# Six re-read buffers and six kept gelus, a shared pool for attention's keys, and row fetches moved between stages of a decoder layer

## The chip, the cores and the metric

The kernel runs on one core of a Trainium2 chip. The metric is the time of one execution on the device, in microseconds (us). Engines are named as in the profile: PE (matrix multiplication), DVE (vector), ACT (activation), POOL (GpSimd) and SP (which here only issues DMAs); POOL issues the indirect DMAs.

## The reference

One layer of a decoder for 512 new tokens of a prompt and 64 tokens of eight running sequences: a gated short convolution and a sliding-window attention, merged through sigmoid gates, layer norm, and then a mixer that picks 128 of 16,384 experts for each token:

```python
def block_fn(xb):                                    # a block of tokens, h
    qv = einsum('nd,de->ne', xb, w_pq).reshape(PEER_BLOCK, 8, 2, 128)
    s = einsum('nhpc,hpkc->nhpk', qv, sub_keys)      # two lists of 128 key scores per head
    top_s, top_i = top_k(s, 16)
    cand_s = top_s[:, :, 0, :, None] + top_s[:, :, 1, None, :]
    cand_i = top_i[:, :, 0, :, None] * 128 + top_i[:, :, 1, None, :]
    best_s, sel = top_k(cand_s.reshape(PEER_BLOCK, 8, -1), 16)
    idx = take_along_axis(cand_i.reshape(PEER_BLOCK, 8, -1), sel)
    gate = softmax(best_s)
    pre = einsum('nd,nhkd->nhk', xb, expert_u[idx])
    coef = gate * gelu(pre)
    return einsum('nhk,nhkd->nd', coef, expert_v[idx])

y = layer_norm(ALPHA * h + peer(h), ln2_g, ln2_b)
```

All arithmetic is in float32; matrix products use a high and a low part of each operand and three products (hi times hi, hi times lo, lo times hi).

## The kernel before

**Tiles.** The 576 token rows lie in chunks of 128: chunk 0 (prompt rows 0 to 127), `SMP` (the 64 sample rows and prompt rows 128 to 191), and chunks 1 to 3 (the other 320 prompt rows). Chunk 0 and `SMP` form the first half, chunks 1 to 3 the second; for the mixer the 64 prompt rows of `SMP` are moved into the free half of chunk 3.

**Two ways through the experts.** For chunk 0 and the 64 sample rows (`GATHER`) the chosen expert rows are fetched: one indirect DMA of 128 rows of 1024 values (512 KB) for each of 192 slots (128 experts for each row of chunk 0, and 64 slots that hold two experts for each sample row), issued by POOL (L512), first 192 from `expert_u`, each followed by a dot product on DVE (L526), then 192 from `expert_v`, each followed by a multiply-add on DVE (L535). `experts()` is a generator; one step issues the fetch that lies `GLAG` steps ahead, into one of `GBUF` row buffers, and does one DVE operation. It is called as side work: `table(..., pace)` loads a 512 KB table on SP (L138), copies the high part on ACT (L119), subtracts it on POOL or DVE to get the low part `wlo` (L120), and, if `pace` is over 0, runs `pace` steps of the generator behind that subtraction. For the other 384 token rows (`DENSE`) all 16,384 experts are computed, in 128 tables. `front(t)` (L856) loads table t of `expert_u`, multiplies it with the transposed activations (24 matmuls of 128x384) and applies gelu on ACT; for t < `NS` the result goes through a tile `sp` to DRAM (`spill`), for later t it is kept in a tile `gel` of `LAG` buffers. `middle(t)` (L898) multiplies it on DVE (L910) with the gate values `gm` (loaded eight tables at a time in three DMAs of 512 KB); for t < `NS` the spilled gelu is first read back into a tile `re` (three buffers, L905); then ACT and DVE make its high and low part, `chi` and `clo`. `back(t)` loads table t of `expert_v`, and 18 matmuls of 128x512 (L940) add to six accumulators in PSUM.

**Stages.** (1) To about 520 us: projections, convolution, attention, merge and first layer norm of both halves, the first half's key scores and routing among them. (2) Scores of the second half, four groups of four `w_pq` tables with top-16 searches and routing on DVE (`route`, with an Exp on ACT, L448), each followed by five fronts (`FQ`), to 780 us. (3) Gate matrices: `hot` tiles (one-hot rows times weights: compare on DVE, L787, scale on ACT, L793, or POOL, L795; matmul L796), with fronts between groups until `AHEAD - KEEP` are done; to about 905 with fronts and to 978 without. (4) The last ten fronts ahead of the sweep (`KEEP`), 978 to 1033. (5) The sweep: steps t < `NS` hold only second products ("solo", to 1290), while `AHEAD` = `NS + LAG` fronts were done ahead; then each step has 18 second-product matmuls and a front's 24 ("paired", to 1777); the fronts run out `LAG` steps before the end, and the rest is solo again (the tail). (6) Second layer norm of chunks 1 to 3 and the output.

**What sets the order.** Nothing moves at run time: the framework simulates the program once and writes each engine's instructions in the order in which that simulation started them, so a change of buffer counts or of paces can move instructions in every queue. SP's queue and POOL's are in that order too. `tc.issue_after` holds an instruction behind another one. The paces are constants: none behind tables of the second half's scores (L586), two or one in turn behind fronts before the sweep (`PACE_U`), none behind fronts in the sweep, one behind each `back` for t < `NS` and three afterwards (`PACE_V`). The first products' low parts are made on POOL before the sweep and on DVE in it; the second products' on DVE for t < `NS` and for t over 124, on POOL between.

## Time and profile before

| | us |
|---|---|
| median of 3 runs (lowest, highest) | 1848.39 (1845.89, 1849.37) |
| the profiled execution | 1850.18 |
| its span in the trace | 1848.4 |
| PE busy (93%) | 1723.9 |
| weight loads on PE, beside matmuls (85%) | 1566.4 |
| DVE busy (79%) | 1464.7 |
| ACT busy (42%) | 781.4 |
| POOL busy (60%) | 1109.6 |

The profiled execution's own time is 1.8 us over its span. The shares are means over stages that are not alike, so the table only says which engine to look at first; the rows below divide the span by stage. The DMA engines moved 496.50 MB, 269 GB/s on the mean, and the granted PE clock was 0.972 of full speed.

### The profile page before, as it was taken

To read this page: it belongs to the slowest core of one execution; us is meant where nothing else is said; L and a number is where in the kernel's file an instruction comes from. 1 tells how busy PE (TensorE), PEld (TensorE's weight loads), DVE (VectorE), ACT (ScalarE), POOL (GpSimd) and SP (SyncE) were. 2 spreads that over 40 slices of the span, in tenths; PEclk is the share of its full clock that TensorE was granted. 3 is DMA by queue.
4 is the path that set the end of the run, shared out by engine and by line. 5 is a ranking of instruction groups with operands and counts; after the bars stand their busy time and mean duration, and the time that the engine had idled before them with its cause. 6 is when DMAs were issued, how large, how long until landed. Compare 5 with 4: busy or idle time off the path is not lost.

```text
span 1848.4 us, 27569 instructions
## 1 busy us (share of the span) xinstructions
PE 1723.9 (93%) x9760; PEld 1566.4 (85%) x9760; DVE 1464.7 (79%) x2588; ACT 781.4 (42%) x1337; POOL 1109.6 (60%) x724
## 2 busy tenths in 40 slices
PE   7999998998799999899888899999999999999985
PEld 7998898988489899799878778778999999999974
DVE  5634579998965699987893778779788878888887
ACT  4554444443233344377794333333333333343322
POOL 4445434367857777798645422224678787778783
PEclk9999999999989999899999999999999999999998
DMA  7446443368757789899748899999999999989873
GB/s 252 134 150 225 138 132 122 115 200 300 249 201 241 235 294 311 271 349 348 289 188 303 317 333 335 336 346 339 333 314 345 337 324 350 353 307 343 314 268 104
DMA packets 190539, 496.50 MB, mean 269 GB/s; under 512 B 17712, under 2 KB 83696, under 8 KB 187312
## 3 DMA queue, kind: packets, MB, share of 16 engines
q1 hardware_dynamic: 135104, 293.39, 46.5%
q0 software_dynamic: 55296, 201.35, 30.2%
q8 instruction: 76, 1.25, 0.3%
q14 instruction: 63, 0.52, 0.1%
HBM read 454.48 MB, written 40.54 MB: 268 GB/s over the span
## 4 chain that ended last, share of the span: by engine, by line
PE 40%; DVE 23%; DMA 14%; issue 9%; POOL 8%; ACT 4%; SPq 1%; DVEq 0%; POOLq 0%; ACTq 0%
PE acc L940 15%; PE ps L123 7%; PE ps L124 7%; PE ps L125 7%; DMA g<-in_ev,idx 5%; POOL wlo L120 4%; POOL g L512 4%; DVE junk L526 3%; PE ps L796 3%; DMA re<-spill 2%; DVE wlo L120 2%; DMA raw<-in_ev 2%; DMA raw<-in_w_o 1%; ACT whi L119 1%; ACT hot L793 1%
## 5 line engine op out<-in xcount | busy, mean ns | idle before, releaser
L120 POOL TENSOR_TENSOR wlo<-raw,whi 128x1024 fp32r<-128x1024 f32 x232 | 579.1, 2499 | 301.8 <-ACT whi L119 264.7
L119 ACT ACTIVATE whi<-raw 128x1024 fp32r<-128x1024 f32 x388 | 409.5, 1056 | 603.9 <-PE ps L124 236.1
L123 PE MATMUL ps<-xhi,whi 128*128 128x384 f32 (+2 forms) x1600 | 529.9, 331 | 21.6 <-ACT sp L863 13.4
L125 PE MATMUL ps<-xhi,wlo 128*128 128x384 f32 (+2 forms) x1600 | 526.1, 329 | 3.5 <-POOL wlo L120 2.0
L124 PE MATMUL ps<-xlo,whi 128*128 128x384 f32 (+2 forms) x1600 | 526.1, 329 | 0.0
L535 DVE SCALAR_TENSOR_TENSOR h<-g,pre,h 128x1024 f32<-128x1024 f32 x192 | 309.8, 1614 | 68.3 <-DMA g<-in_ev,idx 66.8
L512 POOL DMA_INDIRECT g<-in_eu,idx x192 | 204.2, 1063 | 233.1 <-DVE junk L526 186.9
L123 PEld LDWEIGHTS ps<-xhi,whi 128*128 128x128 f32 x1600 | 308.4, 193 | 31.0 <-ACT sp L863 15.1
L512 POOL DMA_INDIRECT g<-in_ev,idx x192 | 257.0, 1338 | 124.9 <-DVE h L535 77.9
L125 PEld LDWEIGHTS ps<-xhi,wlo 128*128 128x128 f32 x1600 | 307.8, 192 | 5.3 <-POOL wlo L120 2.3
L124 PEld LDWEIGHTS ps<-xlo,whi 128*128 128x128 f32 x1600 | 308.3, 193 | 2.9 <-issue 0.3
L940 PE MATMUL acc<-whi,chi 128*128 128x512 f32 x756 | 291.4, 392 | 14.5 <-ACT chi L119 8.2
L940 PE MATMUL acc<-wlo,chi 128*128 128x512 f32 x756 | 296.9, 393 | 7.6 <-POOL wlo L120 7.6
L940 PE MATMUL acc<-whi,clo 128*128 128x512 f32 x756 | 256.4, 392 | 1.1 <-DVE clo L120 1.1
L120 DVE TENSOR_TENSOR wlo<-raw,whi 128x1024 fp32r<-128x1024 f32 x156 | 203.5, 1304 | 46.0 <-ACT whi L119 43.6
L940 PEld LDWEIGHTS acc<-whi,chi 128*128 128x128 f32 x756 | 142.6, 189 | 46.7 <-ACT chi L119 11.5
L940 PEld LDWEIGHTS acc<-wlo,chi 128*128 128x128 f32 x756 | 142.4, 188 | 38.0 <-POOL wlo L120 9.7
L526 DVE SCALAR_TENSOR_TENSOR junk<-g,hp 128x1024 bf16<-128x1024 f32 x104 | 125.9, 1210 | 56.8 <-DMA g<-in_eu,idx 54.8
L940 PEld LDWEIGHTS acc<-whi,clo 128*128 128x128 f32 x756 | 142.4, 188 | 31.3 <-DVE clo L120 1.6
L526 DVE SCALAR_TENSOR_TENSOR junk<-g,h 128x1024 bf16<-128x1024 f32 x88 | 130.9, 1488 | 3.3 <-DMA g<-in_eu,idx 3.0
L796 PE MATMUL ps<-hot 128*128 128x128 f32 x768 | 113.4, 290 | 14.5 <-ACT hot L793 13.4
L787 DVE TENSOR_TENSOR hot<-pt,T 128x1024 f32<-128x1024 f32 x96 | 113.9, 1218 | 15.8 <-PE ps L796 12.7
(250 smaller groups left out, 2157.9 us busy)
## 6 DMA issues: line engine op xcount, KB each, us to landing
raw<-in_euT SPq DMA_DIRECT2D x128, 512.0 KB
raw<-in_ev SPq DMA_DIRECT2D x128, 512.0 KB
gd<-gb SPq DMA_DIRECT2D x24, 1024.0 KB
gm<-gd SPq DMA_DIRECT2D x48, 512.0 KB
raw<-in_w_g SPq DMA_DIRECT2D x32, 512.0 KB
raw<-in_w_pq SPq DMA_DIRECT2D x32, 512.0 KB
raw<-in_w_bch SPq DMA_DIRECT2D x24, 512.0 KB
spill<-sp SPq DMA_DIRECT2D x60, 192.0 KB
```

The lines of the kernel that those rows point to most:

```text
L119: A.activation(hi, src, AF.Copy)
L120: return (eng or V).tensor_tensor(lo, src, hi.bitcast(F32), op=ALU.subtract)
L123: PE.matmul(ps, L[0], R[0], start=start, stop=False)
L124: PE.matmul(ps, L[0], R[1], start=False, stop=False)
L125: PE.matmul(ps, L[1], R[0], start=False, stop=stop)
L512: G.indirect_dma_start(out=rows[i], out_offset=None, in_=I[src], in_offset=bass.IndirectOffsetOnAxis(ap=idx[c][:, s:s + 1], axis=0))
L526: V.scalar_tensor_tensor(junk, g, 1.0, in_psum(c), op0=ALU.mult, op1=ALU.mult, accum_out=p)
L535: V.scalar_tensor_tensor(h_tok[c], g, p, h_tok[c], op0=ALU.mult, op1=ALU.add)
L787: V.tensor_tensor(hot, iota_ps.unsqueeze(1).unsqueeze(1).broadcast_to([128, 2, 4, 128]), T[:, 0:2, n:n + 4].unsqueeze(3).broadcast_to([128 ...
L793: A.activation(oi, oi, AF.Copy, scale=weight_of)
L796: newest[1] = PE.matmul(ps[:, r * 128:(r + 1) * 128], hot[:, 1, r, :], oi, start=True, stop=True).ins
L940: PE.matmul(*args, **kw)
```

## The change

- `NS` 60 to 63 and `LAG` 9 to 6: 63 gelus are spilled and six kept; `AHEAD` stays at 69, so the same fronts run before the sweep, and in the sweep a front runs six tables ahead of its second product. `re` gets six buffers.
- `GBUF` 4 to 5, `GLAG` 2 to 3: five row buffers, fetches three ahead. `OB` 3 to 4: four `hot` buffers.
- Paces: one step behind each `w_pq` table of the second half's scores (`PACE_Q`); three behind each of the last ten fronts before the sweep; for t < `NS` one step behind two of three `back` calls. After `NS` they stay at three.
- `mask_p`, `kT_all` and `v_all` (1, 2 and 2.5 KB a partition) move from the constants to a pool of their own, which is closed after attention, so that later pools can use the room; the scores' `sc` tiles get a pool that is closed before the gate matrices.

```diff
-NS = 60
-LAG = 9
+NS = 63
+LAG = 6
 AHEAD = NS + LAG
-GBUF = 4
-GLAG = 2
+GBUF = 5
+GLAG = 3
...
-OB = 3
+OB = 4
...
-PACE_A, PACE_B, PACE_U, PACE_V = (1, 0), (2, 1, 1), (2, 1), (1, 3)
+PACE_A, PACE_B, PACE_Q, PACE_U, PACE_V = (1, 0), (2, 1, 1), 1, (2, 1), (1, 3)
...
-    mask_p = const("mask_p", [128, 256], src=I["mask_p"])
...
-    kT_all = const("kT_all", [128, SEQ])
-    v_all = const("v_all", [128, 5, 128])
...
         if s.units > LO_N:
-            return table(src, "w", G)
+            return table(src, "w", G, PACE_Q)
...
+    kvs = ExitStack()
+    pools["kv"] = kvs.enter_context(pool("kv", "right"))
+    mask_p, kT_all = tmp("kv", [128, 256], "mask_p"), tmp("kv", [128, SEQ], "kT_all")
+    v_all = tmp("kv", [128, 5, 128], "v_all")
+    loads.insert(0, (mask_p, I["mask_p"]))
...
+    kvs.close()
...
-    pools["b"] = bs.enter_context(pool("b", "right"))
+    pools["b"] = bs.enter_context(pool("b0", "right"))
...
-        wu = table(I["euT"][t], "w", G if t < AHEAD else V, PACE_U[t % len(PACE_U)] if t < AHEAD else 0)
+        wu = table(I["euT"][t], "w", G if t < AHEAD else V, (PACE_U[t % len(PACE_U)] if t < AHEAD - KEEP else 3) if t < AHEAD else 0)
...
+    bs.close()
+    pools["b"] = bs.enter_context(pool("b", "right"))
...
-            ge = tmp("v", [128, ND], "re", bufs=3)
+            ge = tmp("v", [128, ND], "re", bufs=6)
...
-                   PACE_V[t >= NS])
+                   PACE_V[1] if t >= NS else PACE_V[0] * (t % 3 > 0))
```

The change moves line numbers: the dot is L523 after, the fetch L509, the re load L911, the compare L784.

POOL's queue at the end of the sweep, before; each `wlo` is the low part of one second-product table, the last one that of table 124, and each `g<-in_ev` a row fetch:

```order
L512 DMA g<-in_ev,idx_98 128x1024 x3
L120 TENSOR_TENSOR wlo<-raw,whi 128x1024
L512 DMA g<-in_ev,idx_98 128x1024 x3
L120 TENSOR_TENSOR wlo<-raw,whi 128x1024
L512 DMA g<-in_ev,idx_98 128x1024 x3
L120 TENSOR_TENSOR wlo<-raw,whi 128x1024
L512 DMA g<-in_ev,idx_98 128x1024 x3
L120 TENSOR_TENSOR wlo<-raw,whi 128x1024
L512 DMA g<-in_ev,idx_98 128x1024
L120 TENSOR_TENSOR wlo<-raw,whi 128x1024
L512 DMA g<-in_ev,idx_98 128x1024 x3
L120 TENSOR_TENSOR wlo<-raw,whi 128x1024 x2
```

and after, again to table 124:

```order
L509 DMA g<-in_ev,idx_95 128x1024 x3
L120 TENSOR_TENSOR wlo<-raw,whi 128x1024
L509 DMA g<-in_ev,idx_95 128x1024 x3
L120 TENSOR_TENSOR wlo<-raw,whi 128x1024
L509 DMA g<-in_ev,idx_95 128x1024 x3
L120 TENSOR_TENSOR wlo<-raw,whi 128x1024
L509 DMA g<-in_ev,idx_95 128x1024 x3
L120 TENSOR_TENSOR wlo<-raw,whi 128x1024
L509 DMA g<-in_ev,idx_95 128x1024 x2
L120 TENSOR_TENSOR wlo<-raw,whi 128x1024 x4
```

The last fetch stands ahead of the last four tables' subtractions instead of the last two, with two or three fetches in a step up to there. Beside this PE's order has the last front's matmuls ahead of table 118's second products before, and ahead of table 121's after.

POOL's queue around the last group of four `w_pq` tables of the second half's scores, before (the five `wlo` in a row are theirs and that of the front behind them; `g<-in_eu` are row fetches for the dots):

```order
L512 DMA g<-in_eu,idx_95 128x1024
L120 TENSOR_TENSOR wlo<-raw,whi 128x1024
L512 DMA g<-in_eu,idx_95 128x1024 x2
L120 TENSOR_TENSOR wlo<-raw,whi 128x1024 x5
L512 DMA g<-in_eu,idx_95 128x1024
L120 TENSOR_TENSOR wlo<-raw,whi 128x1024
L512 DMA g<-in_eu,idx_95 128x1024 x2
L120 TENSOR_TENSOR wlo<-raw,whi 128x1024
```

and after:

```order
L509 DMA g<-in_eu,idx_92 128x1024 x2
L120 TENSOR_TENSOR wlo<-raw,whi 128x1024
L509 DMA g<-in_eu,idx_92 128x1024
L120 TENSOR_TENSOR wlo<-raw,whi 128x1024
L509 DMA g<-in_eu,idx_92 128x1024
L120 TENSOR_TENSOR wlo<-raw,whi 128x1024
L509 DMA g<-in_eu,idx_92 128x1024
L120 TENSOR_TENSOR wlo<-raw,whi 128x1024
L509 DMA g<-in_eu,idx_92 128x1024
L120 TENSOR_TENSOR wlo<-raw,whi 128x1024
L509 DMA g<-in_eu,idx_92 128x1024
L120 TENSOR_TENSOR wlo<-raw,whi 128x1024
```

A fetch now follows each of these tables, here and in the three groups ahead. On DVE the dots that stand ahead of the first `hot` compare go from 92 to 112 with all that moves, ahead of the last from 128 to 151, and ahead of the third top-16 batch of the second half's scores from 53 to 66. The fetches issued from the last front before the sweep to the first second-product table that POOL splits (table 60, now 63) go from 68 to 56.

SP's queue in the solo part of the sweep, around the fourth block of three `gm` loads, before:

```order
L138 DMA raw<-in_ev 128x1024 x2
L906 DMA re<-spill 128x384 x3
L138 DMA raw<-in_ev 128x1024 x2
L902 DMA gm<-gd 128x8x128 x3
L906 DMA re<-spill 128x384 x2
L138 DMA raw<-in_ev 128x1024
L906 DMA re<-spill 128x384
L138 DMA raw<-in_ev 128x1024 x2
L906 DMA re<-spill 128x384
```

and around the same block after:

```order
L138 DMA raw<-in_ev 128x1024
L911 DMA re<-spill 128x384
L138 DMA raw<-in_ev 128x1024
L907 DMA gm<-gd 128x8x128 x2
L911 DMA re<-spill 128x384
L907 DMA gm<-gd 128x8x128
L138 DMA raw<-in_ev 128x1024
L911 DMA re<-spill 128x384
L138 DMA raw<-in_ev 128x1024
L911 DMA re<-spill 128x384
```

Where that block's first load stands, 25 loads of `expert_v` tables and 17 of `re` have been issued before, 20 and 16 after; at the next block 33 and 26 before, 28 and 24 after. In ACT's order of the ten fronts ahead of the sweep, where the first `expert_v` tables are copied too, five gelus stand ahead of the first two table copies that follow each other directly before, and seven after.

## Rows read from the trace of the kernel before

**Rows 1.** Windows: stretch and length, busy us (instructions) of each engine, PEclk, DMA share, GB/s.

```profile
520.00:625.00 105.00, 104.85 (x649) 101.03 (x649) 53.06 (x225) 37.89 (x55) 76.95 (x46) 1.00 0.73 245
625.00:780.00 155.00, 139.30 (x786) 136.16 (x785) 152.72 (x495) 62.30 (x85) 114.24 (x70) 0.95 0.82 278
...
780.00:905.00 125.00, 123.72 (x832) 123.14 (x831) 104.00 (x128) 90.47 (x219) 108.69 (x100) 0.99 0.95 347
905.00:978.00 73.00, 59.82 (x395) 52.97 (x395) 67.29 (x69) 64.81 (x188) 31.20 (x52) 0.95 0.50 201
978.00:1033.00 55.00, 45.12 (x247) 44.34 (x245) 22.23 (x23) 18.07 (x25) 30.30 (x18) 0.93 0.89 303
1033.00:1290.00 257.00, 248.46 (x1079) 203.47 (x1080) 205.69 (x308) 88.93 (x118) 73.06 (x65) 0.99 0.97 338
1290.00:1777.00 487.00, 487.00 (x2461) 443.07 (x2460) 414.05 (x355) 174.94 (x239) 373.71 (x228) 1.00 0.93 329
1777.00:1848.00 71.00, 44.02 (x183) 33.40 (x182) 56.66 (x67) 18.50 (x28) 37.40 (x22) 0.90 0.48 162
```

**Rows 2.** Chain near 1300 (start us, us, what), then PE's timeline in the tail.

```profile
1295.72 4.12 PE acc L940 x18
...
1304.03 4.12 PE acc L940 x18
...
1777.35 0.39 PE L940 MATMUL acc<-whi,chi 128*128 128x512 f32 x1
...
1830.65 0.39 PE L134 MATMUL acc<-whi,sp 128*128 128x512 f32 x1
```

**Rows 3.** Waits of PE, 1777 to 1832: total us, times, longest us.

```profile
PE acc L940 <- POOL wlo L120: 7.6, 5, 2.9
```

**Rows 4.** Timeline of POOL in the tail: start us, us, instruction [idle before <-releaser].

```profile
1801.15 2.42 POOL L120 TENSOR_TENSOR wlo<-raw,whi 128x1024 fp32r<-128x1024 f32 x1
1803.72 1.76 POOL L512 DMA_INDIRECT g<-in_ev,idx  x1 [0.16 <-issue]
1805.79 1.00 POOL L512 DMA_INDIRECT g<-in_ev,idx  x1 [0.30 <-issue]
1807.09 1.36 POOL L512 DMA_INDIRECT g<-in_ev,idx  x1 [0.30 <-issue]
```

**Rows 5.** Lines by form, 1050 to 1250 (busy us, mean ns | idle before), then PE's waits.

```profile
L940 PE MATMUL acc<-whi,chi 128*128 128x512 f32 x280 | 109.8, 392 | 8.0 <-ACT chi L119 8.0
...
L512 POOL DMA_INDIRECT g<-in_eu,idx x46 | 46.2, 1004 | 149.7 <-DVE junk L526 149.7
L910 DVE TENSOR_TENSOR re<-re,gm 128x384 f32<-128x384 f32 x45 | 24.8, 554 | 27.2 <-DMA re<-spill 27.2
...
PE acc L940 <- ACT chi L119: 8.2, 8, 1.6
```

**Rows 6.** Lines by form, 650 to 780; waits of DVE, 520 to 625; of PE, 620 to 780.

```profile
L526 DVE SCALAR_TENSOR_TENSOR junk<-g,hp 128x1024 bf16<-128x1024 f32 x35 | 42.1, 1203 | 0.0
...
L526 DVE DVE_READ_ACCUMULATOR junk<-g,hp 128x1 f32 x35 | 2.7, 77 | 0.0
...
DVE junk L526 <- DMA g<-in_eu,idx: 50.4, 9, 14.3
...
PE ps L123 <- ACT sp L863: 13.4, 4, 6.3
```

**Rows 7.** Waits of PE, 905 to 1033: total us, times, longest us.

```profile
PE ps L796 <- ACT hot L793: 12.1, 20, 2.4
```

**Rows 8.** Timelines of PE and DVE, 1010 to 1035.

```profile
1012.80 0.69 PE L123 MATMUL ps<-xhi,whi 128*128 128x384 f32 x1 [4.85 <-ACT gel L867]
...
1033.31 0.77 PE L940 MATMUL acc<-whi,chi 128*128 128x512 f32 x1 [5.34 <-ACT whi L119]
...
1014.40 1.92 DVE L910 TENSOR_TENSOR re<-re,gm 128x384 f32<-128x384 f32 x1 [10.17 <-DMA re<-spill]
```

**Rows 9.** Timeline of DVE, 1809 to 1831: the last accumulations of fetched rows.

```profile
1810.13 6.77 DVE L535 SCALAR_TENSOR_TENSOR h<-g,pre,h 128x1024 f32<-128x1024 f32 x3 [2.02 <-DMA g<-in_ev,idx]
```

## The prediction, as put on record

> **What bounds the kernel now.** I read first the busy times by stretch [rows 1]. One engine carries most of the time, PE, and it is not loaded alike everywhere: from 1290 to 1777 us it is busy 487.00 of 487.00 us, so no edit can shorten that stretch without taking matmuls away, and this change takes none. What can move is in six other places. From 625 to 780 DVE is busy 152.72 of 155 us and PE loses 15.7. From 780 to 905 PE is nearly full (123.72 of 125). From 905 to 978 the gate matmuls wait for ACT. From 978 to 1033 ten fronts take 55 us. From 1033 to 1290 PE is busy 248.46 of 257 us beside a DMA share of 0.97. After 1777 PE is busy 44.02 of 71 us. Then I read, for those stretches only, what PE waits for, and last the rows of the engine that it waits for: a wait "on POOL" in the tail is a question of what else POOL does there.
>
> **The tail: gain 11 (3 to 13).** The last front ends at 1777.35 and PE's last matmul at 1831.04 [rows 2]: 53.7 us for ten table steps of second products. A step that nothing hinders is 18 matmuls in 4.12 us [rows 2], ten are 41.2, so 12.5 are lost. The waits name POOL's subtraction for 7.6 of it [rows 3]; the rest goes in smaller stops around those. Why POOL is late stands in its rows: ahead of a subtraction of 2.4 us lie three row fetches of 1.00 to 1.76 us [rows 4], so a step costs POOL about 1.76 + 1.00 + 1.36 + 0.8 between them + 2.4 = 7.3 us, where PE needs 4.12. In the paired stretch PE takes 8.31 us for a step (1304.03 - 1295.72, [rows 2]), and the same 7.3 fit. The change moves exactly this: with LAG 6 the last front stands ahead of table 121 instead of 118, so the run of steps without fronts shrinks from ten to seven, and the order shows the last fetch ahead of POOL's last four subtractions instead of its last two. All steps with three fetches then lie beside fronts. The three steps that leave the tail are not gone: they stand at the head of the sweep (64 solo steps there instead of 61), where POOL splits nothing. Of 12.5 I leave 2 (tables 125 to 127 are split on DVE, and the sample chunk's finish now stands near them in ACT's and DVE's queues) and count the end after PE's last matmul, 17 us of the span, unchanged. Upper end 13, lower end 3 where the finish gets in the way (a rival, below).
>
> **Solo steps with spilled gelus: gain 7 (3 to 9.5).** From 1050 to 1250 one of the three kinds of product ran 280 times [rows 5], six to a step: 46.7 steps in 200 us, 4.286 us each, 0.166 above 4.12. Over 60 steps that is 10. PE's waits there are eight on ACT's chi, 8.2 us together [rows 5], one for every eight steps, which is when three loads of gm (512 KB each) go out on SP's queue. Chi is late because DVE's multiplication waits 27.2 us in that window for re [rows 5], and re's load stands behind gm on the one queue with at most three buffers ahead. With six buffers the order puts more re loads ahead: where the fourth block of gm is issued, 25 ev and 17 re have been issued before, 20 and 16 now, and in the next block 28 and 24; re trails ev by four instead of eight, so each re has about four steps (16 us) more than it had, against 4.7 us for three gm loads at 338 GB/s (1.57 MB). Does the bandwidth carry it? Per step: 512 KB of ev, 192 of re, 192 of gm (1536 over eight steps), and 46 fetches of 512 KB in 46.7 steps [rows 5]: 1400 KB, or 334 GB/s at 4.286 us, against 338 shown. After, 56 fetches are issued in 64 steps instead of 68 in 61 (two in three back steps carry one): 1344 KB per 4.12 us is again 334, and with the bare pace of two in three 1237 KB is 307. So the freed fetches are what pays for the faster step. I take 7 of 10 and not all of it, because the DMA share of 0.97 is a second limit close behind the first.
> The Trainium skill, "Perfetto Trace Analysis", section "Optimization Strategy", says that the same gap repeating on an engine that should be saturated can mean too few buffers for the next tile. By that rule alone the whole 10 would go, and the sum would be -13 in place of -10; no row of before can show it, since the buffers are what changes.
>
> **Scores and gate matrices: loss 6 (0 to 13).** Taking fetches out of the solo stretch means putting their dots somewhere earlier. One fetch now follows each of the w_pq tables that had none, and the order shows the dots ahead of the first hot going from 92 to 112, ahead of the last from 128 to 151. A dot costs DVE 1.203 + 0.077 = 1.28 us [rows 6]. From 520 to 625 DVE is busy 53.06 of 105 us, with 50.4 us waiting for fetched rows [rows 1, 6]; from 625 on it is full. The order has 13 of the new dots ahead of the third top-k batch, about where DVE becomes full; they fill idle time. Seven more come before the first hot (9.0 us) and three among the hots (3.9 us). What DVE is late by reaches PE through ACT: the routing's Exp waits for DVE, a front's gelu waits behind Exp, PE waits for the gelu's bank (four times, 13.4 us in all, 6.3 the longest) [rows 6]. The upper end is 9.0 + 3.9 = 13; the lower is 0, since from 780 to 905 DVE has 21 us idle and PE is the engine that sets the pace. The Exp also moves by one front in ACT's order, so that one more gelu lies ahead of each; that bounds what reaches PE, and I take 6. In the pure gate stretch itself hots come at ACT's pace, and the fourth hot buffer and nine matmuls fewer there (200 for 209) I cost at nothing; what hides it is that PE's 12.1 us of waits are on ACT's scaling [rows 7], and no scaling is removed.
>
> **Ten fronts before the sweep: loss 2 (gain 8 to loss 6).** 24 matmuls at about 0.174 us (8.31 - 4.12 = 4.19 for a front) make ten fronts 41.9 us; they took 55. PE waits 4.85 for a gelu that stands behind a second-product table's copy in ACT's queue, and 5.34 for the first table's copy [rows 8]; DVE waits 10.17 for re [rows 8]. The order now has seven gelus in place of five ahead of the first two copies in a row, for a gain up to 8 of the 10 in those two waits. Against that about four more fetches (3 side steps each on the last ten fronts) bring 2.1 MB, 7 us at 303 GB/s [rows 1], of which the first copy's wait may take six; and three more spills and six re loads ahead of the first ev. No row decides between them; I take 2, near the middle.
>
> **At nothing.** Keys, values and mask in another pool: they are allocated at the same places, and the mask's load is still last of its list. The fifth row buffer and the third row ahead: a fetch is 1.0 us on POOL [rows 5] and goes out earlier, not more often; what it could cost is traffic at another time, on DMA engines with a share of 0.73 up to 625 [rows 1]. The work up to 520 us stays within 3 us either way.
>
> **Sum.** -11 - 7 + 6 + 2 = -10 on the profiled execution's 1850.18 us, or 1840. That execution is the longest of those shown (median 1848.39, 1845.89 to 1849.37), so by the median it is 1838; I say 1839.
>
> **Rivals.**
> 1. Slower: DVE as the bound of scores and gates. If none of the 23 added dots (151 - 128) is hidden, since their rows come as late as those that DVE already waits for, 23 x 1.28 = 29 us reach the path: -11 - 7 + 29 + 2 = +13, 1861. The gains without this term are 16, so it turns the sign from 12.5 dots on PE's path, and measurably from 15. For it: DVE is full for 155 us and every PE wait there ends with ACT behind DVE. Against: 52 us idle just ahead.
> 2. The tail's gain given back. The sample chunk's finish follows the last accumulation (1810.13 to 1816.9, [rows 9]); its table load and scaling now stand in ACT's queue ahead of the copies of tables 123 on. If they wait there, the tail keeps 3 of 11: -2, 1846. Against: the last fetch comes some 15 us earlier relative to PE.
> 3. The DMA engines stay the bound: share 0.97 [rows 1], solo steps keep 8 of 10 (gain 2), and the transition pays its 6: -11 - 2 + 6 + 6 = -1, 1847.
> 4. The solo stretch as an underused PE: weight loads are busy 203.47 of 257 us (79%), where the paired half has 443.07 of 487 (91%) [rows 1]. If the difference were time to be had, 0.12 x 257 = 31 us more would go: 1808. Against: unhindered matmuls of this form go at 4.12 / 18 = 0.229 us in both halves, and a weight load is 203.47 / 1080 = 0.188 us [rows 1], so 82% is all that this form can show. The Trainium skill, "Perfetto Trace Analysis", section "Identifying the Most-Contended Engine", tells to judge PE by the share of weight loads and not of matmuls; by that rule the stretch would have this slack, and the matmul spacing speaks against it.
>
> **How the numbers follow.** The forecast has 0.57, rival 1 0.13, rival 2 0.13, rival 3 0.14, rival 4 0.03. Of the forecast itself the ends of the four terms and the 3 us of the first part, their distances from the values taken added as squares (8, 4, 7, 4 and 3 upward, 2, 2.5, 6, 10 and 3 downward), give 12 either way, 1827 to 1851; the range 1826 to 1856 takes in rivals 2 and 3 and leaves out rival 4 and most of rival 1. A measurement here can tell 0.2% (3.7 us) from no change: faster means under 1844.7. The forecast is faster in nearly all of its cases, rival 4 too; rivals 2 and 3 are mostly the same, with some below; rival 1 and the forecast's upper end are slower or the same: faster 0.59, same 0.23, slower 0.18.
>
> **What would show it.** Right: the stretch from the last front to PE's last matmul falls from 53.7 for ten steps to some 31 for seven, POOL no longer named; chi waits every eight steps vanish, a solo step under 4.18 us; PE's waits on gelu banks in the score stage grow by under 8. Wrong: waits on gelu or hot growing by 20 (rival 1), tail waits on ACT's or DVE's copies of tables 123 to 127 (rival 2), solo steps at 4.25 or more with the gaps spread (rival 3), the transition far from 55 us.

## The result, and the profile after

The changed kernel takes 1867.46 us (median of 4 runs, 1862.58 to 1878.43), the kernel before 1848.56 beside it: a ratio of 1.0113, interval 1.0064 to 1.0162. It is slower, outside the range and on the side of rival 1, but not by rival 1's mechanism. The profiled execution (1862.58 us, span 1860.7) is the shortest of the four, so its 12.3 us over the span of before are a low reading of the 19 us between the medians.

Windows of the changed kernel, in the columns of [rows 1]:

```profile
625.00:780.00 155.00, 140.66 (x791) 137.64 (x790) 154.40 (x503) 62.21 (x83) 121.77 (x77) 0.96 0.88 302
780.00:905.00 125.00, 123.54 (x846) 122.38 (x844) 108.25 (x135) 94.67 (x233) 108.25 (x102) 1.00 0.92 338
905.00:978.00 73.00, 59.76 (x383) 53.66 (x383) 68.36 (x76) 59.70 (x175) 33.71 (x52) 0.93 0.58 231
978.00:1033.00 55.00, 45.45 (x235) 44.49 (x233) 19.79 (x26) 14.84 (x22) 30.72 (x20) 0.88 0.99 346
1033.00:1290.00 257.00, 229.28 (x968) 184.33 (x969) 171.38 (x246) 82.68 (x110) 46.94 (x46) 0.96 0.84 284
1290.00:1777.00 487.00, 485.97 (x2430) 438.13 (x2429) 445.67 (x365) 175.16 (x239) 355.30 (x222) 1.00 0.94 331
1777.00:1860.00 83.00, 68.27 (x325) 58.83 (x323) 58.75 (x72) 28.81 (x41) 34.73 (x20) 0.94 0.40 135
```

Scores and gates stand as before (139.30 against 140.66, 123.72 against 123.54, 59.82 against 59.76 us of PE). The solo stretch does not: PE is busy 229.28 of 257 us against 248.46, and the DMA engines, at 0.97 before, are at 0.84. So more bytes can hardly be what PE waits for there.

The borders of the stages, from PE's timeline (start us, us, instruction); after: the first front behind the last hot, the first second product, the first front in the sweep, the first second product behind the last front, the last matmul:

```profile
976.78 0.42 PE L123 MATMUL ps<-xhi,whi 128*128 128x384 f32 x1
...
1046.83 0.76 PE L945 MATMUL acc<-whi,chi 128*128 128x512 f32 x1 [14.43 <-issue]
...
1325.63 0.34 PE L123 MATMUL ps<-xhi,whi 128*128 128x384 f32 x1
...
1815.73 0.39 PE L945 MATMUL acc<-whi,chi 128*128 128x512 f32 x1
...
1846.31 0.40 PE L134 MATMUL acc<-whi,sp 128*128 128x512 f32 x1
```

and the two of before that are not in [rows 2, 8]:

```profile
978.49 0.42 PE L123 MATMUL ps<-xhi,whi 128*128 128x384 f32 x1
...
1282.66 0.33 PE L123 MATMUL ps<-xhi,whi 128*128 128x384 f32 x1
```

| stage (us) | before | after | change | forecast |
|---|---|---|---|---|
| to the last hot | 978.5 | 976.8 | -1.7 | +6 |
| last hot to first second product | 54.8 | 70.1 | +15.2 | +2 |
| solo steps up to the first front | 249.4 (58) | 278.8 (62) | +29.4, or +12.9 without the four more steps (16.5) | -7 |
| first front to the end of PE's work | 548.4 | 521.1 | -27.3, or -10.8 with those steps | -11 |
| PE's end to the end of the span | 17.4 | 14.0 | -3.4 | 0 |

Counting second products up to the first front (1044 and 1116, 18 to a step) gives 58 and 62 steps, 4.30 and 4.50 us each. So the score term was too pessimistic, the tail was right, and two terms were far off: the fronts ahead of the sweep and the solo steps.

The first second product after waits 14.43 us and the trace names no releaser ("issue", row above). DVE's timeline shows what ends at that moment:

```profile
1045.39 1.22 DVE L523 SCALAR_TENSOR_TENSOR junk<-g,hp 128x1024 bf16<-128x1024 f32 x1 [0.78 <-DMA g<-in_eu,idx]
1046.54 0.08 DVE L523 DVE_READ_ACCUMULATOR junk<-g,hp 128x1 f32 x1
1047.79 1.23 DVE L523 SCALAR_TENSOR_TENSOR junk<-g,h 128x1024 bf16<-128x1024 f32 x1 [1.17 <-DMA g<-in_eu,idx]
```

The last dot that reads `hp` ends at 1046.6, the product starts at 1046.83, and the next dot reads `h`. `hp` is a copy of the activations in PSUM for the dots (`in_psum`); its pool is closed behind the fronts, and the accumulators take the banks. The trace of before has the same picture, although it names ACT there ([rows 8]):

```profile
1031.87 1.22 DVE L526 SCALAR_TENSOR_TENSOR junk<-g,hp 128x1024 bf16<-128x1024 f32 x1
1033.02 0.08 DVE L526 DVE_READ_ACCUMULATOR junk<-g,hp 128x1 f32 x1
...
1034.16 1.22 DVE L526 SCALAR_TENSOR_TENSOR junk<-g,h 128x1024 bf16<-128x1024 f32 x1
```

The last dot on `hp` ends at 1033.1, the product starts at 1033.31. Of the fourteen kernels here whose dots read `hp` up to the sweep, thirteen start the first second product 0.21 to 0.25 us behind the last such dot (e14_re3_hold 0.7 us).

Waits in the solo stretch of after, of PE from 1033 to 1330, then of DVE from 1046 to 1330 (total us, times, longest):

```profile
PE acc L945 <- DVE clo L120: 14.9, 15, 3.6
PE acc L945 <- issue: 14.4, 1, 14.4
...
DVE re L915 <- DMA re<-spill: 80.5, 41, 6.7
```

Before, DVE waited 27.2 us for re in the 200 us of [rows 5]. The 62 steps take 23.4 us more than 62 x 4.12, and the waits for clo are 14.9 of that. Part of the rest is PE's clock. After the standstill of 14.43 us and after two waits of 2.14 and 3.60 us some ten matmuls each follow one another at 0.43 us in place of 0.23, the lower of the clock's two levels (1.2 and 2.4 GHz): about 2 us each time. The granted clock there, in the columns of [rows 1] (mean of a window, 1.00 is full speed):

```profile
1046.80:1052.80 6.00, 5.97 (x17) 4.78 (x18) 2.47 (x4) 0.00 (x0) 3.71 (x3) 0.63 0.96 354
1135.00:1142.00 7.00, 5.89 (x19) 4.72 (x20) 6.85 (x11) 2.54 (x3) 1.23 (x1) 0.76 0.83 288
...
1243.00:1256.00 13.00, 9.40 (x35) 7.26 (x34) 8.12 (x11) 2.55 (x3) 2.50 (x2) 0.87 0.80 271
```

One stop of DVE for re, on DVE, SP and PE:

```profile
1123.89 0.55 DVE L120 TENSOR_TENSOR clo<-re,chi 128x384 fp32r<-128x384 f32 x1
...
1125.09 3.03 SPq L911 DMA_DIRECT2D re<-spill  x1
...
1135.03 0.56 DVE L915 TENSOR_TENSOR re<-re,gm 128x384 f32<-128x384 f32 x1 [6.71 <-DMA re<-spill]
1135.51 0.55 DVE L120 TENSOR_TENSOR clo<-re,chi 128x384 fp32r<-128x384 f32 x1
...
1136.11 1.31 PE L945 MATMUL acc<-whi,clo 128*128 128x512 f32 x3 [2.14 <-DVE clo L120]
```

and what a load takes, from the DMA view of 1060 to 1260 (count, KB, median us to landing):

```profile
raw<-in_ev SPq DMA_DIRECT2D x44, 512.0 KB, 4.6
re<-spill SPq DMA_DIRECT2D x44, 192.0 KB, 4.8
```

DVE stands 6.71 us in front of a multiplication, then makes the clo that PE has waited 2.14 us for. Counted through the sweep, the multiplication is that of step 24, the clo at 1135.51 that of step 20, and the clo at 1123.89 that of step 18, behind which the load was issued. The same pattern some steps earlier, in DVE's order of the changed kernel (re_11241 is step 16, re_11272 step 17; clo_11105 belongs to step 12, clo_11140 to 13, wlo_11212 to table 19):

```
L915 TENSOR_TENSOR re_11241<-re_11241,gm_11237 128x384
L120 TENSOR_TENSOR clo_11105<-re_11101,chi_11104 128x384
L120 TENSOR_TENSOR wlo_11212<-raw_11209,whi_11211 128x1024
L523 SCALAR_TENSOR_TENSOR junk_11217,pre_4189<-g_11079,h4_94 128x1024
L915 TENSOR_TENSOR re_11272<-re_11272,gm_11237 128x384
L120 TENSOR_TENSOR clo_11140<-re_11136,chi_11139 128x384
```

The clo of step 13 stands behind the multiplication of step 17. With six buffers, re of step 17 is loaded into the buffer of step 11, so its load starts only when the clo of step 11 is done. Counted over the whole order: if the last multiplication ahead of clo(t) is that of step m, it needs a load that waits for clo(m - buffers), and the loop closes over t - (m - buffers) steps. Before, one of 60 clo has a loop of one step, 17 of two, 42 of three; after, 29 of 63 have one step and 28 two. With 4.8 us to land and about 1 us for the multiplication and the clo, a loop of one step is longer than the 4.12 us of a step on PE, and one of two steps is shorter than 8.24. It is not where the load of re is issued among three loads of gm, as in the stop shown: from the load's issue to the multiplication it is 9.9 us. Four such stops (steps 24, 32, 48 and 56, all two-step loops) hold 8.5 of PE's 14.9 us, and one-step loops 5.5. So the gm blocks that the prediction named have a part in it; what decides is whether DVE's order makes a clo wait for them.

### The profile page after: what moved, and what is told of

It is laid out like the page before. It is cut to its first block, busy times and chain, and to the rows that moved or that the text cites. A ratio compares the mean times of both kernels' runs of the same rounds, so it can differ in the third digit from the quotient of the medians.

```text
span 1860.7 us, 27665 instructions
## 1 busy us (share of the span) xinstructions
PE 1732.1 (93%) x9760; PEld 1571.8 (84%) x9760; DVE 1484.5 (80%) x2591; ACT 781.7 (42%) x1339; POOL 1090.9 (59%) x721
## 5 line engine op out<-in xcount | busy, mean ns | idle before, releaser
L509 POOL DMA_INDIRECT g<-in_ev,idx x192 | 240.5, 1253 | 173.6 <-DVE h L532 104.4
L123 PEld LDWEIGHTS ps<-xhi,whi 128*128 128x128 f32 x1600 | 308.9, 193 | 29.2 <-ACT sp L866 20.2
L532 DVE SCALAR_TENSOR_TENSOR h<-g,pre,h 128x1024 f32<-128x1024 f32 x192 | 296.9, 1546 | 32.9 <-DMA g<-in_ev,idx 30.4
L509 POOL DMA_INDIRECT g<-in_eu,idx x192 | 206.6, 1076 | 189.0 <-DVE junk L523 148.5
L945 PE MATMUL acc<-whi,chi 128*128 128x512 f32 x756 | 294.2, 392 | 15.1 <-issue 14.4
L945 PE MATMUL acc<-whi,clo 128*128 128x512 f32 x756 | 278.9, 397 | 14.9 <-DVE clo L120 14.9
L523 DVE SCALAR_TENSOR_TENSOR junk<-g,hp 128x1024 bf16<-128x1024 f32 x135 | 163.4, 1210 | 41.4 <-DMA g<-in_eu,idx 39.1
L945 PEld LDWEIGHTS acc<-whi,clo 128*128 128x128 f32 x756 | 141.3, 189 | 51.7 <-DVE clo L120 22.8
L915 DVE TENSOR_TENSOR re<-re,gm 128x384 f32<-128x384 f32 x63 | 39.6, 632 | 109.3 <-DMA re<-spill 109.0
L793 PEld LDWEIGHTS ps<-hot 128*128 128x128 f32 x768 | 105.8, 198 | 20.3 <-ACT hot L790 12.5
```

The costliest lines, as they stand in the source:

```text
L123: PE.matmul(ps, L[0], R[0], start=start, stop=False)
L509: G.indirect_dma_start(out=rows[i], out_offset=None, in_=I[src], in_offset=bass.IndirectOffsetOnAxis(ap=idx[c][:, s:s + 1], axis=0))
L523: V.scalar_tensor_tensor(junk, g, 1.0, in_psum(c), op0=ALU.mult, op1=ALU.mult, accum_out=p)
L532: V.scalar_tensor_tensor(h_tok[c], g, p, h_tok[c], op0=ALU.mult, op1=ALU.add)
L793: newest[1] = PE.matmul(ps[:, r * 128:(r + 1) * 128], hot[:, 1, r, :], oi, start=True, stop=True).ins
L915: V.tensor_tensor(g3, g3, gm[0][:, :, t % IB, :], op=ALU.mult)
```

## The experiments

Ratios are to runs of the kernel before beside them on the same chip; that kernel ran from 1841 to 1866 us in these, so the ratio and the stages of the profiles are used, not the bare times. "Step" is the time from the first second product to the first front in the sweep, divided by the steps in it, as above.

**e1_hold.** The multiplications keep a distance; nothing else changes. The order then has loops of four steps and more.

```diff
-        V.tensor_tensor(g3, g3, gm[0][:, :, t % IB, :], op=ALU.mult)
+        with tc.issue_after(lows[t - 3]) if 3 <= t < NS else ExitStack():
+            V.tensor_tensor(g3, g3, gm[0][:, :, t % IB, :], op=ALU.mult)
...
-        split(co[0], co[1], ge)
+        lows[t] = split(co[0], co[1], ge).ins
```

> The changed kernel with one edit: the multiplication of step t may not stand ahead of the low-part subtraction (clo) of step t - 3 in DVE's order; all loads, buffers and paces stay. Theory (the order on DVE makes a loop: clo of t stands behind a multiplication of t + 5, whose re load got its buffer only when clo of t - 1 was done): DVE's waits for re in the solo stretch fall from 80.5 us to under 30, PE's waits for clo from 14.9 to under 5, the time by 10 to 17 us, to some 1850 to 1857. Rival (the re loads themselves come late, behind gm and ev on SP's queue, whatever DVE's order): waits for re stay above 60 and the time within 5 us of the changed kernel.

Ratio 0.991 (0.9881 to 0.9938), median 1840.41 (1838.82 to 1843.91). Waits of PE, 1025 to 1330:

```profile
PE acc L946 <- issue: 14.2, 1, 14.2
...
PE acc L946 <- DVE clo L120: 0.6, 1, 0.6
```

The waits for clo go from 14.9 to 0.6, DVE's for re from 80.5 to none, a step from 4.50 to 4.13: the solo steps take 256.0 us, 22.8 less. The same loads, buffers and paces with another order on one engine: the loop theory holds, and by more than expected, since the kernel is now faster than the one before. The wait ahead of the sweep stays, as it should. The executions also lie closer together (5 us, 16 in the changed kernel).

**e2_one_each.** One fetch behind every solo step.

```diff
-                   PACE_V[1] if t >= NS else PACE_V[0] * (t % 3 > 0))
+                   PACE_V[1] if t >= NS else PACE_V[0])
```

> The changed kernel with one row fetch behind every back step of the solo stretch, as before, in place of two in three. Theory (fewer dots there let the order run ahead; with one each the order has 1 clo in a one-step loop where the changed kernel has 29): PE's waits for clo under 8, the time 8 to 15 us below the changed kernel, about 1853. Rival (DMA bytes decide): the stretch gets slower by what 64/3 more fetches of 512 KB cost, up to 30 us of traffic; not below the changed kernel.

Ratio 0.9959 (0.9925 to 0.9993). Its order has one one-step loop in 63; a step takes 4.19. More work on DVE makes the stretch shorter, because it changes the order. By the ratios it is some 28 us below the changed kernel, about twice what was expected.

**e3_re3.** Three buffers in the changed kernel.

```diff
-            ge = tmp("v", [128, ND], "re", bufs=6)
+            ge = tmp("v", [128, ND], "re", bufs=3)
```

> The changed kernel with three re buffers as before; paces and the rest as changed. Theory (the order's loop, not the depth): its order still has 28 of 63 steps whose clo waits for a load released one step before, so the solo stretch stays slow, PE waits there of 12 us or more, time 1860 to 1872. Rival (six buffers are what hurts): waits go back to the 8 us of before, time some 1852.

Ratio 1.0098 (1.0057 to 1.0139), as slow as the changed kernel. Waits of PE, 1025 to 1330, and of DVE, 1040 to 1310:

```profile
PE acc L945 <- DVE clo L120: 14.5, 11, 2.4
...
DVE re L915 <- DMA re<-spill: 80.3, 38, 6.7
```

The six buffers are not the cause; its order has 28 one-step loops with three.

**e4_hp_off.** The dots from the last ten fronts on read SBUF.

```diff
-        if "hp" not in pools:
+        if "hp" not in pools or done >= AHEAD - KEEP:
```

> The changed kernel, in which the dots issued from the last ten fronts on read the activations from SBUF instead of their copy in PSUM (the bank that the accumulators take over). Theory: PE's 14.4 us wait ahead of the first second product ends when the last dot on that bank ends, so it falls to under 6 (the wait for table copies is next), and the time falls by 8 to 12 us, more if the order of the solo stretch gets better with it. Rival (the extra fetches hold up the first tables' loads): the wait stays above 10.

Ratio 0.9936 (0.9903 to 0.9968). PE's waits, 1025 to 1330:

```profile
PE acc L945 <- DVE clo L120: 7.9, 5, 4.5
PE acc L945 <- ACT whi L119: 2.7, 2, 1.3
```

The 14.4 us wait is gone: the first second product starts at 1039.4, as the last front ends (1039.5). From last hot to there it is 53.9 us against 70.1. The order of the solo stretch changed with it (9 one-step loops), a step takes 4.35.

**e5_hold_hp.** The edits of e1_hold and e4_hp_off together.

> The changed kernel with both edits: a multiplication held behind the clo of three steps before, and the dots from the last ten fronts on reading SBUF in place of the PSUM copy. If the two losses are separate, the gains add: PE's wait ahead of the first second product under 6 us, waits for clo under 2, and a time of 1828 to 1834. If the wait ahead of the sweep only moves (to table copies, since the loads come late), the time stays at 1838 to 1842.

Ratio 0.9885 (0.9863 to 0.9908), median 1833.99. More than either alone, less than the sum (0.991 and 0.9936 against 1.0113 would give some 0.974): a wait of 6.3 us for a table's copy comes up in the solo stretch.

**e6_two_of_three.** The pace of two in three in the kernel before, alone.

```diff
-                   PACE_V[t >= NS])
+                   PACE_V[1] if t >= NS else PACE_V[0] * (t % 3 > 0))
```

> The kernel before with one edit: a row fetch behind two of three back steps in the solo stretch in place of every one. Theory: its order has 23 of 60 clo in a one-step loop (1 before), so the stretch slows with three buffers and the old NS: PE's waits on chi or clo there 12 us or more, time 6 to 15 us above the kernel before. Rival (fewer fetches relieve the DMA engines): PE's waits under 8.2, time at or below the kernel before, apart from the fetches' later end.

Ratio 1.0286 (1.025 to 1.0322). Waits of PE, 1020 to 1330, and of DVE, 1040 to 1290:

```profile
PE acc L940 <- DVE clo L120: 16.6, 9, 3.9
...
DVE re L910 <- DMA re<-spill: 79.3, 37, 7.7
```

A step goes from 4.30 to 4.54, 14 us over 59 steps: the pace alone makes the loop, with three buffers and the old NS. The rest, which was not expected at this size, is at the end: 19 fetches stand behind POOL's last subtraction, PE ends at 1846.1 and the span at 1893.9.

**e7_ns63.** NS and LAG in the kernel before, alone.

```diff
-NS = 60
-LAG = 9
+NS = 63
+LAG = 6
```

> The kernel before with NS 63 and LAG 6 alone (three re buffers, old paces). Theory of the tail: the steps without fronts at the end go from ten to seven and POOL's late subtractions with fetches lie beside fronts, so from the last front to PE's last matmul 53.5 us fall to some 34, of which 12.4 go to the head of the sweep: 7 to 12 us faster than before. Rival (the finish of the sample chunk takes the place of the fetches): under 4 us faster.

Ratio 0.9992 (0.9964 to 1.0019): no difference. Waits of PE from 1330 on:

```profile
PE acc L940 <- POOL wlo L120: 6.0, 4, 2.3
```

From the end of the last front's last matmul to PE's end it is 36.1 us, 17.4 less than before (53.5) where 12.4 move to the head of the sweep: a gain of 5. The end behind PE grows from 17.4 to 20.2, and most of the waits on POOL stay (7.6 in [rows 3]). POOL's waits, 1770 to 1850 (the last front ends at 1792):

```profile
POOL g L512 <- DVE h L535: 3.2, 5, 0.7
```

**e8_pace_u.** The old paces behind the last ten fronts in the changed kernel.

```diff
-(PACE_U[t % len(PACE_U)] if t < AHEAD - KEEP else 3) if t < AHEAD else 0)
+PACE_U[t % len(PACE_U)] if t < AHEAD else 0)
```

> The changed kernel with the old paces (two and one in turn) behind the last ten fronts before the sweep. Theory: the 15 steps fewer end the dots on the PSUM copy earlier, so PE's wait ahead of the first second product falls from 14.4 to 4 to 8 us; its order has 16 one-step loops for 29, so the waits for clo fall to some 8; time 8 to 15 us below the changed kernel. If the wait ahead of the sweep comes from spills and re loads instead, it stays above 12.

Ratio 0.9964 (0.9943 to 0.9985). From last hot to first second product 49.3 us, 21 less than in the changed kernel and 5.5 less than before; the waits for clo are 8.2 us. PE waits 1.14 us ahead of the first second product, less than expected, and the time falls by more (28 us by the ratios). So the three fetches behind each of those fronts cost 21 us in that place. Taking them out costs at the end: five fetches stand behind POOL's last subtraction, and behind PE's end come 24.5 us in place of 14.0.

**e9_best and e10_u_hold.** The held order with the old paces ahead of the sweep; e9_best with one fetch behind every solo step, e10_u_hold with two in three. These are the edits of e1_hold and e8_pace_u, in e9_best that of e2_one_each too.

> The changed kernel with the old paces behind the last ten fronts, one fetch behind every solo step, and the multiplications held behind the clo of three steps before. If the three losses found so far are separate (dots on the PSUM copy and fetches ahead of the sweep, the loop in DVE's order, fetches left for the end), PE's wait ahead of the first second product is under 8, waits for clo under 2, the tail 31 us for seven steps, time 1820 to 1830. If one fetch per step at a full pace is too much for the DMA engines (1400 KB per 4.12 us, 348 GB/s), the solo stretch takes over 264 us for 64 steps and the time is 1832 or more.

> As e9_best, but with two fetches in three solo steps as in the change. Same gains ahead of the sweep and in it; its order leaves five fetches behind POOL's last subtraction, so the tail's end grows: time from PE's last matmul to the end 20 us or more (14 in the changed kernel, 24.5 in e8_pace_u), 1824 to 1834. If bytes bind in e9_best, this one is faster than it.

Ratios 0.986 (0.9828 to 0.9892) and 0.985 (0.9811 to 0.9889), medians 1828.47 and 1829.72. A step takes 4.30 in e9_best, 4.11 in e10_u_hold; behind PE's end come 14.1 and 25.1 us. PE's waits of e9_best from 1017 to 1291, then a stretch in the columns of [rows 1]:

```profile
PE acc L946 <- ACT whi L119: 8.0, 6, 3.2
...
1060.00:1260.00 200.00, 193.47 (x833) 157.40 (x832) 155.26 (x223) 67.95 (x92) 56.61 (x45) 0.98 0.97 333
```

and the same stretch of e10_u_hold:

```profile
1060.00:1260.00 200.00, 200.00 (x884) 165.68 (x883) 148.30 (x222) 75.59 (x100) 35.24 (x34) 1.00 0.93 314
```

With a fetch in every step the DMA engines are full and PE waits for tables (the stretch takes 273 us, as the expectation's second case has it, and the time is in the range of the first); with two in three PE does not wait, and the fetches that were saved come due at the end. So e10_u_hold is not faster than e9_best, as it was expected to be where bytes bind.

**e13_four_of_five.** e10_u_hold with four fetches in five solo steps.

```diff
-PACE_V[0] * (t % 3 > 0))
+PACE_V[0] * (t % 5 > 0))
```

> As e10_u_hold with four fetches in five solo steps (51 of 64 steps in place of 43). Theory (the end is set by the fetches that are left, and the solo stretch by bytes only above some 330 GB/s): the time from PE's last matmul to the end falls from 25 to some 16, the solo stretch stays within 5 us of the 254.7 of e10_u_hold; time 4 to 9 us below it. If the stretch is byte-bound from there on, it grows by 6 or more and nothing is won.

Ratio 0.9847 (0.9789 to 0.9905), median 1822.57, the lowest of all; as a ratio it can't be told from e10_u_hold. In the profiles the solo steps take 255.8 us against 254.7, and PE's end to the span's end is 14.0 against 25.1. Its window:

```profile
1060.00:1260.00 200.00, 199.52 (x879) 164.56 (x878) 154.42 (x229) 74.13 (x100) 46.24 (x40) 1.00 0.96 329
```

The fetches that are left set the end, and eight more of them find room in the solo steps.

**e14_re3_hold.** e10_u_hold with three re buffers (the edit of e3_re3) and a distance of one step (loops of three steps).

```diff
-        with tc.issue_after(lows[t - 3]) if 3 <= t < NS else ExitStack():
+        with tc.issue_after(lows[t - 1]) if 1 <= t < NS else ExitStack():
```

> As e10_u_hold with three re buffers, each multiplication held behind the clo of the step before (63 three-step loops). If what counts is how many steps lie between a buffer's release and the clo that waits for its next load, three suffice: the solo stretch is within 4 us of e10_u_hold, and six buffers are worth nothing beyond that. If the blocks of gm need the depth, PE's waits on chi return to 8 us in the stretch.

Ratio 0.9854 (0.9797 to 0.9911); a step takes 4.11, the solo stretch 254.9 us. A window of this kernel, in the columns of [rows 1]:

```profile
1060.00:1260.00 200.00, 198.68 (x876) 163.94 (x875) 142.53 (x213) 74.22 (x98) 31.76 (x32) 1.00 0.94 316
```

Three buffers do nearly what six do (200.00 us of PE in e10_u_hold).

**e11_before_hold.** The kernel before with the edit of e1_hold, at a distance of one step.

> The kernel before with each multiplication held behind the clo of the step before (its order then has 60 three-step loops, where it has 17 two-step ones). If the loop explains the kernel before too, its 8.2 us of waits on chi fall under 4 and the time by 3 to 8 us. If three buffers behind gm's loads explain them, they stay at 8.

Ratio 0.9979 (0.9959 to 0.9998), waits on chi 6.6 us against 8.2. Little, and not the fall that was expected: before, the loop was not the cause. At one fetch per step the DMA share is 0.99 here.

**e12_before_q.** One fetch behind each w_pq table in the kernel before.

```diff
         if s.units > LO_N:
-            return table(src, "w", G)
+            return table(src, "w", G, 1)
```

> The kernel before with one fetch behind each w_pq table of the second half's scores. Theory (the tail's waits go when the fetches end earlier, not when fewer steps are left without fronts): its order has the last fetch ahead of POOL's last eight subtractions, PE's waits on POOL after the last front fall from 7.6 to under 2 with ten steps there, time 6 to 12 us faster. If the added dots bind in the scores, PE's waits on gelu banks there grow by over 8 and the time stays.

Ratio 0.9954 (0.9927 to 0.9982). Waits of PE from 1320 on:

```profile
PE acc L940 <- POOL wlo L120: 5.6, 4, 2.7
PE acc L940 <- ACT whi L119: 2.4, 1, 2.4
```

The time is as expected, the waits nearly: behind the last front (1778.6) PE waits 2.7 of these 5.6 us for POOL, where before has 7.6. What is left comes together between 1780 and 1790, with the 2.4 us for ACT's copy of a table, which stands behind the finish of the sample chunk. ACT's timeline (the first line is the finish):

```profile
1783.70 1.51 ACT L551 ACTIVATE h<-h,nm,mv 64x512 f32<-64x512 f32 x2
...
1785.52 1.05 ACT L119 ACTIVATE whi<-raw 128x1024 fp32r<-128x1024 f32 x1
```

From the last front to PE's end it is 49.3 us (53.5 before), and behind PE's end 14.0 (17.4): some 4 and 3. PE's waits on gelu banks in the scores did not grow (6.9 us against 13.4).

**e15_before_hp.** The edit of e4_hp_off in the kernel before.

> The kernel before, in which the dots from the last ten fronts on read SBUF in place of the PSUM copy. Theory (before, too, the first second product waits for the last dot on that bank): PE's 5.3 us wait there falls under 3, 2 to 5 us faster. If it waits for the first table's copy, as the profile of before has it, nothing changes.

Ratio 1.0014 (0.9987 to 1.0041). The first second product starts as the last front ends (1033.3 and 1033.5), so the 5.3 us wait of before was for the dots and not for the first table's copy. Nothing is won by it in time. In this profile the place itself takes 48.2 us from last hot to first second product (54.8 before), but the gate matrices ended at 985.4 instead of 978.7, and from the last front to PE's end it takes 58.4 us (53.5), with 11.6 us of waits on POOL (7.6). Why was not tried; the first of the two may be no more than the difference between executions (e1_hold, e2_one_each and e3_re3, whose edits lie behind the gate matrices, reach the last hot at 982.5, 974.6 and 980.5).

## Why the prediction was wrong, point by point

**The fronts ahead of the sweep** (forecast +2, measured +15.2). The step that failed is the reading of [rows 8]: the 5.34 us ahead of the first second product were put down to ACT's copy, as the row has it, and the term was bounded by what moves in ACT's queue. DVE's timeline of before, above, and e15_before_hp show that PE waited there for the last dot on the PSUM copy. Three fetches behind each of ten fronts put eight more dots into that place (15 in place of 7 behind 960 us), nine of them behind 1030 (two before). Of the 15.2 us 9.1 are this wait (14.43 against 5.34). The other 6.1 are the ten fronts themselves, 55.6 us against 49.5. PE's waits among them, 968 to 1047 of after:

```profile
PE ps L123 <- ACT sp L866: 5.5, 1, 5.5
PE ps L125 <- POOL wlo L120: 3.4, 1, 3.4
```

This part fits the traffic that the prediction counted (about four more fetches, 7 us): while the fronts run 12 fetches are issued against 9 before, and the DMA share from 978 to 1033 is 0.99 against 0.89. That the traffic is what slows them was not tried alone. e8_pace_u prices the pace: 21 us, 13.3 by the wait and 7.5 by the fronts (48.1 us); e4_hp_off takes the wait away by the bank alone. The other part of the term, a gain in ACT's queue, is not shown: of the 5.5 us that e8_pace_u gains on before, 4.2 are the wait for the dots.

**Solo steps** (forecast -7, measured +12.9). Two steps failed. The first is that six buffers give re four more steps of lead. That was counted in SP's queue, where it is true; but the multiplication moved forward by as much in DVE's queue, and an instruction that stands early in a queue holds what stands behind it. e1_hold shows it (order alone: 4.50 to 4.13 a step), e3_re3 and e6_two_of_three that depth has no part in it: three buffers give the same loop with the pace of two in three, and e14_re3_hold that three suffice without it. The second: which part of the change moves the order. It is the pace (e2_one_each takes the one-step loops from 29 to 1, e6_two_of_three brings 23 into the kernel before). Why it does is argued and not shown: with fewer dots the simulated DVE is free sooner, and the scheduler places multiplications as early as the buffers let it. The bandwidth sum was right on its own: at two in three the held order runs at 4.11, at one in one at 4.30 with a full DMA share (e9_best), so the freed fetches are what pays, as the prediction said, and not the buffers.

The Trainium skill, "Perfetto Trace Analysis", section "Optimization Strategy", says that the same gap repeating can mean too few buffers for the next tile. These traces do not bear it out: the waits are 14.9 us with six buffers and 14.5 with three (e3_re3), and with a held order a step takes 4.11 us with six and with three; by the rows it is the order, not the space.

**Scores and gates** (forecast +6, measured -1.7). The added dots are hidden, as far as the trace can tell; the term was mis-sized. The kernels e1_hold, e2_one_each and e3_re3 run the same instructions in the same order as the changed one up to there and reach the last hot at 974.6 to 982.5, so one profile's -1.7 tells little more than that no large loss is seen; the waits tell more. PE's waits in the scores after, 620 to 795:

```profile
PE ps L123 <- ACT sp L866: 11.3, 3, 5.3
PE ps L750 <- ACT qv L747: 3.0, 1, 3.0
```

are 14.3 us with both, against 13.4 for the first before. Rival 1 is wrong by its mechanism, though its time is near. e12_before_q has the same dots in the kernel before and even shorter waits.

**The tail** (forecast -11, measured -10.8 and another -3.4 at the end). The size was right, the cause only in part. PE's waits after, from 1320 on:

```profile
PE acc L945 <- POOL wlo L120: 0.8, 1, 0.8
PE acc L945 <- ACT whi L119: 0.6, 1, 0.6
```

are all that is left of it. But NS and LAG alone give 5 and lose 2.8 of it at the end (e7_ns63), earlier fetches alone give 7 (e12_before_q); the change has both. Earlier fetches are not needed, though: e8_pace_u and e10_u_hold have five fetches behind POOL's last subtraction and still take 30.9 and 31.3 us from the last front's end to PE's end, as after (30.8), where e7_ns63 takes 36.1. Something else in the change helps, too. One candidate is the fifth row buffer with the third row ahead, which the prediction put at nothing: in the 17 us up to the end of the last front POOL's fetches wait for DVE in e7_ns63 (row above), and in these three they do not. It was not tried alone, so how the gain divides stays open. The finish of the sample chunk (rival 2) does stand in the way in e12_before_q, not after.

**Rivals 3 and 4.** The DMA engines were not the bound of the solo stretch after (0.84); they are in e9_best. Rival 4 is out: PE at 200.00 of 200 us in the solo steps of e10_u_hold has weight loads at 83%, and no time is left there.

**Versions that beat both kernels.** e13_four_of_five at 0.9847 of the kernel before; e10_u_hold, e14_re3_hold, e9_best and e5_hold_hp are within its interval.

## What to carry to other kernels

When buffers are added or side work is taken away under a scheduler that fixes the order, look on each engine at what now stands ahead of the critical instruction, and count how many steps lie between the release of the buffer that it waits for and its own step; a loop must be shorter than the steps that it spans, also where other loads stand beside its own. A wait that the trace ascribes to nothing ("issue"), or to an engine that was done long ago, can be for a buffer or a bank: look which instruction on any engine ended just then and what it read. Fetches that are taken out of one stage must be placed: price the stage that receives them, and the end.

## What the runs showed of the hardware that was not expected

Between PE full and PE waiting for bytes lies little: from 1060 to 1260 us the traffic of the solo steps was 314 GB/s in e10_u_hold and 329 in e13_four_of_five, with PE at 200.00 and 199.52 us, and 333 in e9_best, which asks for 348 (1400 KB per 4.12 us), with PE at 193.47. And a re load of 192 KB takes 4.8 us to land beside the other loads at a DMA share of 0.82 (1060 to 1260 us of after), no less than a table's 512 KB at 4.6 (rows above): its size does not set that time here. What does was not tried.
